# Heads' loop of two hybrid layers: a hand-written TensorE order and clamps on one engine

## Chip, core and metric

One core of one Trainium2 chip runs the whole program once. The metric is device microseconds of that core, median of several runs. TensorE is called PE below, VectorE DVE, ScalarE ACT, GpSimd POOL and the SyncE queue SP, as the profile names them.

## What is computed

The program is one transformer block followed by two "hybrid" layers, on 512 tokens of width 1024, all in float32. The change touches the state-space half of the hybrid layers only. Cut to that:

```python
def hybrid_layer(x, w_in, ...):
    q, k, v, z_attn, z_ssm, xbc, dt_raw = split(x @ w_in)
    attn = sliding_window_attention(q, k, v, sinks) * silu(z_attn)
    xs, bm, cm = split(silu(causal_depthwise_conv(xbc, conv_w, conv_b)))
    dt = softplus(dt_raw + dt_bias)
    y = ssd_chunked(xs, dt, -exp(a_log), bm, cm) + xs * d_skip
    ssm = gated_rmsnorm(y, z_ssm, ssm_norm_w)
    return layer_norm(ALPHA * x + concat(attn, ssm) @ w_out)

def ssd_chunked(xs, dt, a, bm, cm):          # 4 chunks of 128 tokens, 2 groups of 8 heads
    a_cs = cumsum(dt * a)                    # within a chunk
    xdt = xs * dt
    y_diag = (cm @ bm.T * exp(segsum(a_cs))) @ xdt
    states = bm.T @ (exp(a_cs[-1] - a_cs) * xdt)
    prev = scan(prev * exp(a_cs[-1]) + states)
    y_off = (cm @ prev) * exp(a_cs)
    return y_diag + y_off
```

## The kernel before

Activations lie transposed, channels on partitions and 512 tokens along the free axis. A product of one 128-channel output block ("unit") with the 1024-wide input is made in float32r with each operand split into a high and a low part: `proj` (L185) calls `mm3` (L142), 8 blocks x 3 = 24 PE products of 128x512 into one PSUM bank of the pool "mm" (4 banks): 16 with the high weights (L149, L150), then 8 with the low ones (L154). `weights` (L100) fetches a unit's 512 KB through SP (L104), casts it on ACT (`whi`, L107) and makes the rest on DVE in two pieces (`wlo`, L110); raw, high and low buffers are three each.

`hybrid` (L882) runs once per layer. `conv(j)` is one unit whose bank ACT copies into a tile "ht" (L900), DVE adds three shifted terms to (L902), ACT takes the tanh of (L211) and DVE combines (L905). `silu` (L908) is an ACT tanh and one DVE instruction (L911). Stages in order: four gates `zs` (half of them, for heads 0 to 7), dt, the convolutions of B and C, conv 0 and 1, the masked products `cb`, conv 2, 3 and 4, then the part at issue:

- `tokens(g)` (L1001), once for each group g of heads: for each of four chunks, four PE transposes into a bank "tr" (2 banks; L1007), two DVE products of that bank (`xdt` L1010, `xe` L1014), and, but for the last chunk, a state update: two full-precision float32 passes of 128x512 on PE into a bank "lg" (2 banks; L1016), for chunk 0 an ACT copy (L1019), else two DVE instructions (L1021, L1022). `xe` uses the two tiles "ht" that `conv` uses too.
- `decay_rows(j)` (L1025) issues four SP transfers that spread rows of cumulated sums from a scratch in HBM over partitions. That scratch is written by two transfers of the ACT queue (L951, L953).
- `decay(j)` (L1043), for each pair of heads j: per head four 128-wide clamps and one exponential (L1058), then a product with `cb` (L1059, first head on POOL, second on DVE). The clamp is an ACT Relu (L1057); for the first head of pairs 3 to 7 it is a DVE tensor_scalar (L1055), 20 of them in a layer.
- `heads(j)` (L1062): 16 PE products of 64 columns each (L1070) and 6 of 128 (L1076) into two banks "tr", then three DVE instructions (L1078 to L1080).
- The loop (L1094): for each j it fetches the weights of the next unit of `fill` (L1038), makes one unit (conv 5 to 7, then four gates), issues `decay(j + 1)`, `tokens(1)` at j = 3, `heads(j)`, the gating product (L1110), at j = 6 `gated_norm(0)` (L1082; a norm reduction on PE, L206, then L1087 and splits), and the sum of squares (ACT L199, POOL L200).

After the loop come two units of keys, the values (L1139 to L1141), `gated_norm(1)` and the attention.

The engines work through their queues in order. Who stands where in a queue is laid out at build time by a scheduler that takes what it reckons ready, earlier code first; only SP is kept in the order of the code (`manual_schedule`, L1312). So before the change the order of PE, too, is the scheduler's.

Of the kernel before, what the change touches and what calls it, by code (L numbers as in the profile page):

```python
# [11 lines left out]
ALU = mybir.AluOpType  # L12

P = 128
# [47 lines left out]
class Kern:  # L62
# [79 lines left out]
    def mm3(self, out, w, xs, m=P, start=True, stop=True, woff=0):  # L142
# [9 lines left out]
        for k, (xh, xl) in enumerate(xs):  # L152
            c = slice(woff + k * m, woff + (k + 1) * m)
            nc.tensor.matmul(out, wlo[:, c], xh, start=False, stop=stop and k == n - 1)  # L154

# [726 lines left out]
    def hybrid(self, L):  # L882
# [12 lines left out]
        def conv(j, tag, w=None):  # L895

            y, o = self.f("ht"), self.f(tag)
            cw = lambda w: cwh[:, w * 12 + j : w * 12 + j + 1]
            pt = self.proj(W[4 + j], h, w=w)
# [101 lines left out]
        def tokens(g):  # L1001

            for c in range(4):
                cc = slice(c * P, (c + 1) * P)
                ptx = self.ps("tr")
                for j in range(4):
                    nc.tensor.transpose(ptx[:, j * P : (j + 1) * P], xs[4 * g + j][:, cc], self.ident)  # L1007
                xdt[g, c] = self.f("G")
                o = c * 16 + 8 * g
                nc.vector.tensor_tensor(d3(xdt[g, c]), d3(ptx), bc(dtok, o), ALU.mult)  # L1010
                if c == 3:
                    break
                xe = self.f("ht")
                nc.vector.tensor_tensor(d3(xe), d3(ptx), bc(dend, o), ALU.mult)  # L1014
                pst = self.ps("lg")
                nc.tensor.matmul(pst, bt[c][:, g * P : (g + 1) * P], xe, start=True, stop=True)  # L1016
                prev = self.f("R")
                if c == 0:
                    nc.scalar.copy(prev, pst)  # L1019
                else:  # L1020
                    nc.vector.tensor_tensor(d3(prev), d3(prevs[g, c - 1]), bc(cdec, o), ALU.mult)  # L1021
                    nc.vector.tensor_tensor(prev, prev, pst, ALU.add)  # L1022
                prevs[g, c] = prev
# [10 lines left out]
        for j in range(2, 4):  # L1034
            xs.append(conv(j, "G"))
        xs.append(conv(4, "G"))

        fill = [9, 10, 11, 28, 29, 30, 31]  # L1038
        wn = self.weights(W[fill[0]])
        rows = [decay_rows(0), decay_rows(1)]  # L1040
        tokens(0)

        def decay(j):  # L1043

            dfs, ee = rows.pop(0)
            if j < 6:
                rows.append(decay_rows(j + 2))
# [46 lines left out]
        for j in range(8):  # L1094
            g = j // 4
            w = wn
            if j < 6:
                wn = self.weights(W[fill[j + 1]])
# [330 lines left out]
```

## Time and profile before

| | |
|---|---|
| median of 3 runs | 1650.42 us (1649.81 to 1650.58) |
| the profiled execution | 1650.6 us, its span 1648.8 us |
| PE busy | 1601.2 us, 97% of the span |
| DVE / ACT / POOL busy | 1140.7 / 805.5 / 212.4 us (69 / 49 / 13%) |
| mean granted clock of PE | 0.994 of full speed |

A PE instruction's recorded time runs to the end of its pipeline and overlaps the next one's, so what a product costs is read from start to start, not from its duration; a busy share near 100% can hide waiting.

In the rows further down, a row of busy time by stretch gives the stretch, its length, then the busy us and instruction counts of PE, PE's weight load, DVE, ACT and POOL, PE's granted clock, and the share and GB/s of the DMA engines. A row of a group gives line, engine, operation, names out<-in, shapes and count, then busy us and mean ns of one, then the engine's idle time before them and what ended it. A row of one line's durations gives min/median/max ns, and the first and last start. A row of the timeline gives start, length, and in brackets the idle time before.

### The profile page before, as it was taken

What the parts mean: (1) busy time and instruction counts of PE and PEld (TensorE: products, weight loads), DVE (VectorE), ACT (ScalarE), POOL (GpSimd) and SP (SyncE); (2) the same over time, 40 slices, a digit from 0 to 9 for tenths busy, and PEclk for the clock granted to TensorE, in tenths of its full rate; (3) what the DMA queues carried; (4) which work ended last, traced back from release to release, by engine and by line L of the source; (5) the groups of instructions that cost most, each with busy time, mean ns of one, the idle gap of its engine ahead of it and who ended that gap; (6) DMA issues with size and microseconds to landing.
All of it is one profiled execution on the core that took longest, in us unless ns stands there. A gap on an engine that the chain in (4) does not pass through costs nothing. (4 is left out here: it accounts for less than half of the span.)

```text
span 1648.8 us, 24498 instructions
## 1 busy us (share of the span) xinstructions
PE 1601.2 (97%) x9014; PEld 1358.7 (82%) x9014; DVE 1140.7 (69%) x2490; ACT 805.5 (49%) x1571; POOL 212.4 (13%) x251
## 2 busy tenths in 40 slices
PE   8999999999999999999999999999999989999996
PEld 5778888889898888888998778887998867888786
DVE  6779967547886455533767998765497799777447
ACT  4543245336863333323556556665355555666424
POOL 2000213000100000000000121211230022111131
PEclk9999999999999999999999999999999999999998
DMA  6522332243233323234636223211452522322133
GB/s 222 198 97 76 120 103 64 77 158 116 81 116 111 102 92 100 89 104 119 196 124 191 80 77 103 78 65 51 141 171 81 178 87 78 102 78 65 64 103 116
DMA packets 66233, 180.28 MB, mean 109 GB/s; under 512 B 7953, under 2 KB 19169, under 8 KB 66113
## 3 DMA queue, kind: packets, MB, share of 16 engines
q1 hardware_dynamic: 56320, 166.75, 31.8%
q10 hardware_dynamic: 9792, 11.96, 2.4%
q8 instruction: 71, 1.16, 0.3%
q14 instruction: 50, 0.40, 0.1%
HBM read 170.14 MB, written 9.06 MB: 109 GB/s over the span
## 5 line engine op out<-in xcount | busy, mean ns | idle before, releaser
L149 PE MATMUL psmm<-G,whi 128*128 128x512 f32 (+2 forms) x1244 | 479.2, 388 | 2.2 <-ACT whi L107 2.2
L110 DVE TENSOR_TENSOR wlo<-wraw,whi 128x512 fp32r<-128x512 f32 x515 | 358.8, 718 | 174.8 <-ACT whi L107 123.8
L150 PE MATMUL psmm<-G,whi 128*128 128x512 f32 (+2 forms) x1244 | 473.6, 384 | 0.0
L107 ACT CAST whi<-wraw 128x1024 fp32r<-128x1024 f32 (+3 forms) x262 | 267.7, 1024 | 339.7 <-PE psmm L150 272.3
L154 PE MATMUL psmm<-G,wlo 128*128 128x512 f32 (+2 forms) x1244 | 299.5, 382 | 0.0
L149 PEld LDWEIGHTS psmm<-G,whi 128*128 128x128 f32 (+1 forms) x1244 | 233.3, 188 | 50.3 <-issue 3.5
L150 PEld LDWEIGHTS psmm<-G,whi 128*128 128x128 f32 (+1 forms) x1244 | 233.2, 188 | 45.3 <-issue 1.5
L154 PEld LDWEIGHTS psmm<-G,wlo 128*128 128x128 f32 (+1 forms) x1244 | 228.2, 187 | 45.0
L149 PE MATMUL psmm<-R,whi 128*128 128x256 f32 (+1 forms) x684 | 210.4, 329 | 0.0
L150 PE MATMUL psmm<-R,whi 128*128 128x256 f32 (+1 forms) x684 | 210.1, 328 | 0.0
L149 PEld LDWEIGHTS psmm<-R,whi 128*128 128x128 f32 x684 | 130.0, 190 | 11.8 <-issue 0.3
L150 PEld LDWEIGHTS psmm<-R,whi 128*128 128x128 f32 x684 | 130.0, 190 | 11.5
L154 PE MATMUL psmm<-R,wlo 128*128 128x256 f32 (+1 forms) x684 | 130.3, 329 | 0.0
L154 PEld LDWEIGHTS psmm<-R,wlo 128*128 128x128 f32 x684 | 106.2, 190 | 11.5
L200 POOL TENSOR_TENSOR acc<-acc,sq 128x512 f32<-128x512 f32 (+1 forms) x42 | 53.0, 1261 | 475.4 <-ACT sq L199 475.3
L1176 ACT ACTIVATE w<-w,st 128x256 f32<-128x256 f32 (+1 forms) x128 | 59.9, 470 | 29.3 <-DVE st L1174 29.3
L211 ACT ACTIVATE sq<-ht 128x512 f32<-128x512 f32 (+1 forms) x48 | 29.4, 613 | 60.8 <-DVE ht L902 30.0
L902 DVE SCALAR_TENSOR_TENSOR ht<-psmm,cwh,ht 128x511 f32<-128x511 f32 (+2 forms) x72 | 53.4, 742 | 5.8 <-ACT ht L900 4.6
L836 DVE TENSOR_TENSOR sq<-psmm,G 128x512 f32<-128x512 f32 (+1 forms) x24 | 15.5, 646 | 56.0 <-PE psmm L154 56.0
L1172 DVE CUSTOM_DVE_ANT_0 w<-pslg,w,sinks 128x256 f32<-128x256 f32 (+1 forms) x128 | 51.5, 444 | 1.1 <-PE pslg L1167 0.6
L199 ACT ACTIVATE sq<-G 128x256 f32<-128x256 f32 (+1 forms) x76 | 35.1, 463 | 34.3 <-DVE G L1264 25.9
L1181 POOL TENSOR_SCALAR w<-w,st 128x256 f32<-128x256 f32 x64 | 37.9, 604 | 86.8 <-DVE st L1179 79.0
(332 smaller groups left out, 2597.3 us busy)
## 6 DMA issues: line engine op xcount, KB each, us to landing
wraw<-w_in SPq DMA_DIRECT2D x112, 512.0 KB, 3.4
wraw<-w_out SPq DMA_DIRECT2D x56, 512.0 KB, 3.8
wraw<-w_down SPq DMA_DIRECT2D x24, 512.0 KB, 3.5
wraw<-w_gate SPq DMA_DIRECT2D x22, 512.0 KB, 3.4
wraw<-w_up SPq DMA_DIRECT2D x22, 512.0 KB, 3.4
R<-acs SPq DMA_DIRECT2D x32, 256.0 KB, 5.7
wraw<-w_down SPq DMA_DIRECT2D x12, 384.0 KB, 3.7
wraw<-w_proj_attn SPq DMA_DIRECT2D x8, 512.0 KB, 3.4
```

Source lines behind the costliest of these rows:

```text
L107: nc.scalar.copy(hi[:, :n], raw[:, :n])
L110: nc.vector.tensor_tensor(lo[:, c], raw[:, c], hi[:, c].bitcast(F32), ALU.subtract)
L149: nc.tensor.matmul(out, whi[:, c], xh, start=start and k == 0, stop=False)
L150: nc.tensor.matmul(out, whi[:, c], xl, start=False, stop=False)
L154: nc.tensor.matmul(out, wlo[:, c], xh, start=False, stop=stop and k == n - 1)
L199: self.last_sq = nc.scalar.activation(t, src, AF.Square)
L200: (eng or nc.gpsimd).tensor_tensor(acc, acc, t, ALU.add)
L211: self.last_tanh = self.nc.scalar.activation(out, src, AF.Tanh, scale=scale)
L902: nc.vector.scalar_tensor_tensor(y[:, s:], pt[:, : S - s], cw(3 - s), y[:, s:], ALU.mult, ALU.add)
L1172: nc.vector.tensor_tensor_reduce(pr, pt, al[:, 256 - n :], 1.0, sink, ALU.add, ALU.max, mx[:, b : b + 1])
L1176: nc.scalar.activation(prs[b], prs[b], AF.Exp, bias=nm[:, b : b + 1], accum_out=sm[:, b : b + 1])
L1181: (nc.gpsimd if b % 2 else nc.vector).tensor_scalar(prs[b], prs[b], rc[:, b : b + 1], 1.0, ALU.mult, ALU.mult)
```

## The change

The loop becomes one stretch in which PE's order is that of the code. `unit` and `stream` hand out the 24 products of each of nine units (conv 4 to 7, four gates, the first unit of keys) one by one; `feed(n)` places n of them between a chunk's transposes (`tokens(g, c)`), its state update (`state(g, c)`) and the heads (`step(j)`). The clamps of `decay` are ACT Relus throughout. `xe` moves from tiles "ht" to tiles "rs" (two). Weights are fetched one unit ahead at the start of each unit; `decay_rows` are issued three pairs ahead, after `heads(j)`, and the first of them before the weights of conv 2. The products themselves, their number and their operands are the same.

```diff
@@ -152,6 +152,22 @@
         for k, (xh, xl) in enumerate(xs):
             c = slice(woff + k * m, woff + (k + 1) * m)
             nc.tensor.matmul(out, wlo[:, c], xh, start=False, stop=stop and k == n - 1)
+
+    def unit(self, w, xs):
+
+        whi, wlo = w
+        pt = self.ps()
+
+        def products():
+            n = len(xs)
+            for p in range(3 * n):
+                k = p // 2 if p < 2 * n else p - 2 * n
+                c = slice(k * P, (k + 1) * P)
+                lhs, rhs = (whi, xs[k][p % 2]) if p < 2 * n else (wlo, xs[k][0])
+                self.nc.tensor.matmul(pt, lhs[:, c], rhs, start=p == 0, stop=p == 3 * n - 1)
+                yield
+
+        return pt, products()
 
     def begin(self):
 
@@ -892,11 +908,12 @@
         cwh = self.s("cwh", (P, 60))
         nc.vector.tensor_scalar(cwh, self.vec[:, cw0 : cw0 + 60], 0.5, None, ALU.mult)
 
-        def conv(j, tag, w=None):
-
+        def conv(j, tag, pt=None):
+
+            if pt is None:
+                pt = self.proj(W[4 + j], h)
             y, o = self.f("ht"), self.f(tag)
             cw = lambda w: cwh[:, w * 12 + j : w * 12 + j + 1]
-            pt = self.proj(W[4 + j], h, w=w)
             nc.scalar.activation(y, pt, AF.Identity, scale=cw(3), bias=cwh[:, 48 + j : 49 + j])
             for s in (1, 2, 3):
                 nc.vector.scalar_tensor_tensor(y[:, s:], pt[:, : S - s], cw(3 - s), y[:, s:], ALU.mult, ALU.add)
@@ -998,29 +1015,31 @@
         xdt = {}
         prevs = {}
 
-        def tokens(g):
-
-            for c in range(4):
-                cc = slice(c * P, (c + 1) * P)
-                ptx = self.ps("tr")
-                for j in range(4):
-                    nc.tensor.transpose(ptx[:, j * P : (j + 1) * P], xs[4 * g + j][:, cc], self.ident)
-                xdt[g, c] = self.f("G")
-                o = c * 16 + 8 * g
-                nc.vector.tensor_tensor(d3(xdt[g, c]), d3(ptx), bc(dtok, o), ALU.mult)
-                if c == 3:
-                    break
-                xe = self.f("ht")
-                nc.vector.tensor_tensor(d3(xe), d3(ptx), bc(dend, o), ALU.mult)
-                pst = self.ps("lg")
-                nc.tensor.matmul(pst, bt[c][:, g * P : (g + 1) * P], xe, start=True, stop=True)
-                prev = self.f("R")
-                if c == 0:
-                    nc.scalar.copy(prev, pst)
-                else:
-                    nc.vector.tensor_tensor(d3(prev), d3(prevs[g, c - 1]), bc(cdec, o), ALU.mult)
-                    nc.vector.tensor_tensor(prev, prev, pst, ALU.add)
-                prevs[g, c] = prev
+        def tokens(g, c):
+
+            cc = slice(c * P, (c + 1) * P)
+            ptx = self.ps("tr")
+            for j in range(4):
+                nc.tensor.transpose(ptx[:, j * P : (j + 1) * P], xs[4 * g + j][:, cc], self.ident)
+            xdt[g, c] = self.f("G")
+            o = c * 16 + 8 * g
+            nc.vector.tensor_tensor(d3(xdt[g, c]), d3(ptx), bc(dtok, o), ALU.mult)
+            if c < 3:
+                xe[c] = self.f("rs")
+                nc.vector.tensor_tensor(d3(xe[c]), d3(ptx), bc(dend, o), ALU.mult)
+
+        def state(g, c):
+
+            o = c * 16 + 8 * g
+            pst = self.ps("lg")
+            nc.tensor.matmul(pst, bt[c][:, g * P : (g + 1) * P], xe.pop(c), start=True, stop=True)
+            prev = self.f("R")
+            if c == 0:
+                nc.scalar.copy(prev, pst)
+            else:
+                nc.vector.tensor_tensor(d3(prev), d3(prevs[g, c - 1]), bc(cdec, o), ALU.mult)
+                nc.vector.tensor_tensor(prev, prev, pst, ALU.add)
+            prevs[g, c] = prev
 
         def decay_rows(j):
 
@@ -1031,31 +1050,16 @@
                 nc.sync.dma_start(ee[64 * e_ : 64 * e_ + 64, P:], row[1:, P:].broadcast_to([64, S - P]))
             return dfs, ee
 
-        for j in range(2, 4):
-            xs.append(conv(j, "G"))
-        xs.append(conv(4, "G"))
-
-        fill = [9, 10, 11, 28, 29, 30, 31]
-        wn = self.weights(W[fill[0]])
-        rows = [decay_rows(0), decay_rows(1)]
-        tokens(0)
-
         def decay(j):
 
             dfs, ee = rows.pop(0)
-            if j < 6:
-                rows.append(decay_rows(j + 2))
             for e_, df in enumerate(dfs):
                 hd = 2 * j + e_
-                cut = e_ == 0 and j >= 3
                 for c in range(4):
                     cc = slice(c * P, (c + 1) * P)
                     at = atok[:, c * 16 + hd : c * 16 + hd + 1]
-                    if cut:
-                        nc.vector.tensor_scalar(df[:, cc], df[:, cc], at, 0.0, ALU.subtract, ALU.min)
-                    else:
-                        nc.scalar.activation(df[:, cc], df[:, cc], AF.Relu, bias=at, scale=-1.0)
-                nc.scalar.activation(df, df, AF.Exp, scale=1.0 if cut else -1.0)
+                    nc.scalar.activation(df[:, cc], df[:, cc], AF.Relu, bias=at, scale=-1.0)
+                nc.scalar.activation(df, df, AF.Exp, scale=-1.0)
                 (nc.vector if e_ else nc.gpsimd).tensor_tensor(df, df, cb[hd // 8], ALU.mult)
             return dfs, ee
 
@@ -1088,24 +1092,44 @@
                 cat[8 + i] = self.pair(t, "R")
 
 
+        fill = [8, 9, 10, 11, 28, 29, 30, 31, 0]
+        evict = [lambda pt, j=j: xs.append(conv(j, "G", pt)) for j in range(4, 8)]
+
+        def gate_evict(pt):
+            zs.append(self.f("R"))
+            silu(zs[-1], pt)
+
+        evict += 4 * [gate_evict] + [lambda pt: keys(pt)]
+        ahead = []
+
+        def stream():
+            for u, e in enumerate(evict):
+                pt, products = self.unit(ahead.pop(0), h)
+                if fill:
+                    ahead.append(self.weights(W[fill.pop(0)]))
+                for i, _ in enumerate(products):
+                    if i == 3 * KD - 1:
+                        e(pt)
+                    yield
+
+        fillers = stream()
+
+        def feed(n):
+            for _ in range(n):
+                next(fillers)
+
+
         cat = [None] * 16
         accs = []
-        ws = decay(0)
-        for j in range(8):
-            g = j // 4
-            w = wn
-            if j < 6:
-                wn = self.weights(W[fill[j + 1]])
-            if j < 3:
-                xs.append(conv(5 + j, "G", w))
-            elif j < 7:
-                zs.append(self.f("R"))
-                silu(zs[-1], self.proj(None, h, w=w))
-            nxt = decay(j + 1) if j < 7 else None
-            if j == 3:
-                tokens(1)
-            heads(j, *ws)
-            ws = nxt
+        ws = []
+
+        def step(j):
+
+            if j < 7:
+                ws.append(decay(j + 1))
+            heads(j, *ws.pop(0))
+            if j < 5:
+                rows.append(decay_rows(j + 3))
             y = xs[j]
             nc.vector.tensor_tensor(y, y, zs[j], ALU.mult)
             if j == 6:
@@ -1117,14 +1141,47 @@
 
         top, bot = slice(0, 64), slice(64, P)
         kt = []
-        for j in range(2):
-            pt = self.proj(W[j], h)
+
+        def keys(pt):
             ks = [[self.r("G") for _ in range(2)] for _ in range(2)]
             for (kh, kl), r, o in zip(ks, (top, bot), (bot, top)):
                 self.split(pt[r], kh[r], kl[r], 0.125)
                 for t in (kh, kl):
                     nc.scalar.dma_start(t[o].bitcast(F32), t[r].bitcast(F32))
             kt.append(ks)
+
+        xe = {}
+        rows = [decay_rows(0)]
+        for j in range(2, 4):
+            xs.append(conv(j, "G"))
+        ahead.append(self.weights(W[fill.pop(0)]))
+        rows += [decay_rows(1), decay_rows(2)]
+        ws.append(decay(0))
+        with self.tc.manual_schedule(engines={mybir.EngineType.PE}):
+            for g, lead in ((0, 20), (1, 20)):
+                feed(lead)
+                tokens(g, 0)
+                tokens(g, 1)
+                feed(10 - 2 * g)
+                state(g, 0)
+                tokens(g, 2)
+                feed(6)
+                state(g, 1)
+                tokens(g, 3)
+                feed(8 - 2 * g)
+                state(g, 2)
+                if g == 0:
+                    for n, j in ((8, 0), (24, 1), (22, 2)):
+                        feed(n)
+                        step(j)
+                else:
+                    for n, j in ((0, 3), (10, 4), (22, 5), (22, 6), (22, 7)):
+                        feed(n)
+                        step(j)
+                    feed(2)
+
+
+        keys(self.proj(W[1], h))
         vs = [self.f("G") for _ in range(2)]
         pv = [self.ps("mm") for _ in range(2)]
         for c in range(2):
```

## Rows read from the trace of the kernel before

**Rows 1.** Busy time by stretch: both layers' loops, then the first loop's middle

```profile
905.50:993.56 88.06, 81.20 (x464) 62.60 (x463) 80.93 (x135) 47.20 (x88) 21.62 (x14) 1.00 0.27 82
1309.97:1397.81 87.84, 81.34 (x465) 62.66 (x463) 80.90 (x132) 46.59 (x86) 20.44 (x14) 1.00 0.26 82
...
921.94:977.29 55.35, 50.83 (x300) 38.98 (x300) 54.10 (x96) 31.86 (x61) 13.73 (x9) 1.00 0.29 87
```

**Rows 2.** Waits of PE, first loop (905.50 to 993.56): total us, times, longest

```profile
PE pslg L1016 <- DVE ht L1014: 3.1, 2, 1.9
PE pstr L1007 <- DVE G L905: 1.6, 1, 1.6
PE pstr L1070 <- DVE G L1078: 1.2, 2, 0.9
PE psmm L149 <- ACT whi L107: 0.5, 1, 0.5
```

**Rows 3.** Timeline of PE in the first layer: start us, us, what, count, idle before

```profile
905.50 0.39 PE L149 MATMUL psmm<-G,whi 128*128 128x512 f32 x1
...
910.94 1.03 PE L1007 MATMUL pstr<-ident,G 128*128 128x128 f32 x8
...
911.73 0.48 PE L149 MATMUL psmm<-G,whi 128*128 128x512 f32 x1
...
917.04 1.06 PE L1016 MATMUL pslg<-ht,G 128*128 128x512 f32 x2
...
917.94 0.49 PE L1007 MATMUL pstr<-ident,G 128*128 128x128 f32 x3
...
921.94 1.10 PE L1016 MATMUL pslg<-ht,G 128*128 128x512 f32 x2 [1.87 <-DVE ht L1014]
...
962.55 1.09 PE L1070 MATMUL pstr<-R,G 128*64 128x128 f32 x16
...
964.26 0.47 PE L149 MATMUL psmm<-G,whi 128*128 128x512 f32 x1
...
969.92 1.09 PE L1070 MATMUL pstr<-R,G 128*64 128x128 f32 x16
...
1005.07 1.02 PE L206 MATMUL pstr<-acc,ones 128*128 128x512 f32 x2
1005.53 0.79 PE L149 MATMUL psmm<-G,whi 128*128 128x512 f32 x1
```

**Rows 4.** Groups, one line's durations, and timeline: DVE splits and clamps, a POOL product

```profile
L110 DVE TENSOR_TENSOR wlo<-wraw,whi 128x512 fp32r<-128x512 f32 x20 | 15.2, 785 | 0.9 <-ACT sq L199 0.9
...
L1055 DVE TENSOR_SCALAR R<-R,dtt 128x128 f32<-128x128 f32 x20 | 8.3, 439 | 0.0
...
L1055 DVE TENSOR_SCALAR R<-R,dtt x40: 269/280/1410, 931.4 to 1372.3; 128x128 f32<-128x128 f32 x40
...
936.28 1.28 DVE L1055 TENSOR_SCALAR R<-R,dtt 128x128 f32<-128x128 f32 x1
...
936.18 1.30 POOL L1059 TENSOR_TENSOR R<-R,R 128x512 f32<-128x512 f32 x1 [12.06 <-ACT R L1058]
```

**Rows 5.** ACT and POOL groups of the first loop

```profile
L107 ACT CAST whi<-wraw 128x1024 fp32r<-128x1024 f32 x10 | 10.3, 1042 | 4.0 <-PE psmm L150 4.0
L1057 ACT ACTIVATE R<-R,dtt 128x128 f32<-128x128 f32 x31 | 10.1, 389 | 0.0
L1058 ACT ACTIVATE R<-R 128x512 f32<-128x512 f32 x14 | 8.7, 626 | 3.1 <-DVE R L1055 2.9
...
L211 ACT ACTIVATE R<-psmm 128x512 f32<-128x512 f32 x4 | 2.4, 595 | 5.0 <-PE psmm L154 5.0
...
L1059 POOL TENSOR_TENSOR R<-R,R 128x512 f32<-128x512 f32 x7 | 9.9, 1412 | 36.8 <-ACT R L1058 36.8
```

**Rows 6.** Queues ahead of the first loop: the scratch's write, conv 2's first product

```profile
873.10 0.31 ACTq L953 DMA_DIRECT2D acs<-G  x1
...
894.23 0.48 PE L149 MATMUL psmm<-G,whi 128*128 128x512 f32 x1
```

## The prediction

> **What bounds the kernel now.** I first read the page's busy shares: PE is busy 97% of the span, so the time changes only where PE waits or where its work shrinks. This change alters no product, so I looked for waiting inside that 97%. The busy time by stretch [rows 1] shows the two loops as the places: 88.06 us in the first layer, from the end of conv 3's products to the first product of the values, and 87.84 us in the second. In both, DVE is busy 80.9 us, ACT about 47, POOL about 21. In the first loop's middle, 921.94 to 977.29, DVE is busy 54.10 of 55.35 us: there it is DVE that sets the pace, and PE, in order, stands behind it. The granted clock is 1.00 in all three rows, so no loss is the clock's.
>
> Then the waits of PE [rows 2]: state updates wait 3.1 us for `xe` from DVE, a transpose 1.6 us for conv 7's last DVE instruction, heads 1.2 us for DVE to leave a bank, one unit 0.5 us for ACT's cast. That is 6.4 us, but recorded durations overlap, so I worked out the loop's clean length from start to start [rows 3]. A unit of 24 products takes 910.94 - 905.50 = 5.44 us; eight transposes 911.73 - 910.94 = 0.79; a state update 917.94 - 917.04 = 0.90; a pair's heads 964.26 - 962.55 = 1.71; the norm reduction 1005.53 - 1005.07 = 0.46. The loop has 10 units (54.4), 32 transposes (3.2), 6 state updates (5.4), 8 pairs (13.7) and one reduction (0.5): 77.2 us. So 88.06 - 77.2 = 10.9 us is not products, in the second layer 10.6.
>
> Not all of this is waiting. A run of products that follows other work is longer than its count: 23 products took 917.04 - 911.73 = 5.31 us where 23 x 0.227 = 5.21, 24 after heads took 969.92 - 964.26 = 5.66 where 5.44 is clean [rows 3]. I take 0.16 for such a re-entry, the middle of 0.10 and 0.22. I count 12 in the loop now, 1.9 us; about 9 us a layer are waits.
>
> **The change part by part.**
>
> *PE's order.* By the feed counts, PE has 20 products (4.5 us) between conv 3's end and the first transposes, 10 (then 8 in group 1) between the first two chunks' transposes and the first state update, then 6 and 8 (6) before the next ones; about 22 before each pair, except 8 before pair 0, none before 3 and 10 before 4. Conv 7 ends at product 96, its transposes come after product 118 and pair 2: 22 x 0.227 + 1.71 = 6.7 us lie between, where none lay before and PE waited 1.6. The 1.87 us wait before the third state update [rows 3] gets 8 products, 1.8 us, in front of it. Pairs 0, 1 and the start of 2 ran back to back, which is the heads' wait of 1.2 us; now 24 and 22 products stand between. So the places that wait get cover. The price is more re-entries: I count 15 instead of 12, 2.4 us.
>
> The finer mixing has a rule against it. The Trainium skill (TensorEngine Tiling (Array Packing), Key Properties) says that a change of tiling mode drains TensorE, and heads write 64-partition halves. The rows above agree in sign, 0.22 us behind heads against 0.10 behind transposes, and the sum is made with their mean.
>
> *Clamps.* 20 clamps a layer leave DVE. They are busy 8.3 us, mean 439 ns, while their median over both layers is 280 ns [rows 4]: 20 x (439 - 280) = 3.2 us is stretch. One row shows why: a clamp of 1.28 us starts 0.1 us into a POOL product of 1.30 us and ends with it [rows 4]. So DVE is relieved of 5.1 us at least (if the stretch lands on its other instructions) and 8.3 at most; I take 7. In the loop's middle, where all 20 stand, 54.1 - 7 = 47.1 us of DVE work then stand beside six units, 16 transposes, four state updates and six pairs on PE, 32.6 + 1.6 + 3.6 + 10.3 = 48.1, with re-entries 49: DVE has less to do than PE there, by little.
>
> The Trainium skill (SBUF — State Buffer, Who interferes with whom) lets a tensor_scalar in a two-port mode and any DVE instruction with two SBUF inputs contend with a POOL instruction that reads SBUF. By it POOL's work keeps blocking other DVE instructions, and the relief would be the 5.1; the splits' mean of 785 ns here [rows 4] agrees with such blocking.
>
> *ACT.* It takes 20 Relus at 10.1 / 31 = 0.33 us [rows 5], 6.5 us a layer, on an engine busy 47 of 88 us [rows 1]. In the gate phase a pair costs ACT eight Relus (2.6), two exponentials at 0.62 (1.2), a cast (1.0), a tanh (0.6) and a square like it (0.6): 6.0 us against PE's 22 x 0.227 + 1.71 + 0.16 = 6.9. It fits, without room for disorder; I cost it at nothing, hidden behind those products. If the cover fails, a pair waits for the chain of the slower rival below.
>
> *Tiles, queues, fetches.* `xe` no longer shares the tiles "ht" with conv's accumulator, which only removes waits; I count nothing, since its wait cannot be told from DVE's. On SP the four transfers of `decay_rows(0)` move ahead of the weights of convs 2 to 4, and wait for the scratch that ACT's queue writes at 873.10 [rows 6]. Conv 2's products start at 894.23 [rows 6], 21 us later; four transfers, the fetch, cast and split stay well inside that: nothing. Inside the loop weights are asked for one unit (over 5.4 us) ahead behind four transfers at most. The order of ACT, DVE and POOL is again laid out by the scheduler, now around another PE order; that is bounded by nothing saved on one side and no waits left on the other, 10.9 us a layer apart, and I take the value worked out next.
>
> *What is left waiting.* In group 0, from the first transposes to the last state update, PE offers half of the transposes (1.6), 24 products (5.4) and two state updates (1.8): 8.8 us. DVE has there seven token products, conv 4's four instructions, one state's two and a unit's two splits, 15 instructions at some 0.65 us from start to start (the recorded means here are 0.68 to 0.79 and overlap by about 0.1): 9.8. So about 1 us is short; group 1 has two or four products less and a gate instead of a conv, and pair 3 follows at once: about 1 again. I take 2.2 us with the 0.2 of the rest.
>
> **Sum.** A loop takes 77.2 + 2.4 + 2.2 = 81.8 us: 6.3 less in the first layer (88.06 - 81.8), 6.0 in the second, 12.3 together. The profiled execution took 1650.6 us (span 1648.8), so 1638.3; the median of the runs is 0.2 lower, 1650.4, and gives 1638.
>
> **Rivals.** A measurement of this kernel can tell about 0.2%, 3.3 us, from no change.
>
> *DVE remains the wall.* If POOL's blocking moves over to other instructions and DVE keeps the 7.1 us that it idles in the loop now, the loop is 88.06 - 5.1 = 83.0 us at best, and with a split or a state late once more, 84: gains of 4 to 5 a layer, 1640.5 to 1643; down to 2 a layer, 1646.5, when the idle grows. For it: 98% busy in the middle. Against: 5.9 of its 7.1 idle us lie outside the middle (80.93 - 54.10 = 26.8 busy of 88.06 - 55.35 = 32.7 [rows 1]), where PE mostly had no need of it.
>
> *The waits only move.* The scheduler lays out ACT and DVE anew, and each of 6 state updates and 8 pairs waits 0.5 to 0.8 us: 7 to 11 us a layer, no gain, 1648 to 1653. For it: PE's queue is now rigid, where the scheduler had put ready work ahead. Against: every place of rows 2 gets products in front.
>
> *Slower: ACT's queue becomes the pacer.* Where a tanh that waits for a unit's last product stands in ACT's queue ahead of the Relus of the next pair, that pair's heads wait for tanh (0.6), Relus and exponentials (3.8) and the POOL product (1.4 [rows 5]): 5.9 us, less the products between. Units end at products 168 and 192, pairs 5 and 6 stand at 170 and 192, so the cover is 0 to 0.5 us. Two such places cost 11 us a layer against 6.2 saved: +5 each, about 1660. It decides from about one and a half places a layer. For it: the Relus moved over are those of exactly these pairs. Against: decay of a pair comes a whole step earlier in the code. The Trainium skill (ScalarE: Activation LUTs, Rules for kernel authors) tells authors to put relu and min on VectorE; the rows agree that the clamp is shorter there (a median of 280 ns [rows 4] against a mean of 389 on ACT [rows 5]), but ACT is the engine that has time.
>
> **How the numbers follow.** The forecast (1632 to 1640.5) has 0.52; DVE as the wall (1640.5 to 1646.5) 0.25; waits moved 0.10; slower 0.13. Small gains under 3.3 us fall in the third. So faster 0.77, same 0.10, slower 0.13. The low end: no waits and re-entries at 0.10 give 77.2 + 1.5 = 78.7 us a loop, 9.4 and 9.1 less, 1632. The high end takes in DVE as the wall and most of the waits moved, 1650.
>
> **What would show it.** In the changed profile, each loop should be about 82 us from conv 3's last product to the first of the values, with PE's waits for `xe` and L905 nearly gone, no L1055, and DVE busy some 74 us, under 95% in the middle. Runs of products behind heads should again be 0.1 to 0.2 us long. Wrong would be: heads waiting for POOL's or DVE's product of L1059 (ACT late), a unit waiting for its cast, or stretched two-input DVE instructions that make up for the clamps.

## The result, and the profile after

The change makes the kernel slower: the median goes from 1650.12 us (1649.33 to 1650.58, 4 runs) to 1660.38 us (1658.59 to 1661.57, 4 runs), a ratio of 1.0062, 95% interval 1.0044 to 1.0079. Forecast was 1638, range 1632 to 1650. The profiled execution after took 1658.59 us, span 1656.8.

The hybrid layer is best cut in three pieces. The first runs from conv-B/C's mask products (L979 before, L996 after) to the end of conv 3's products: the lead-in, which holds conv 2 and 3. The second is the loop, to the first product of the values; the third is the rest. The lead-in before, which [rows 1] do not hold, and then the pieces after, as busy time by stretch (start and end, length, then busy us and instructions of PE, PEld, DVE, ACT and POOL, PE's granted clock, DMA share and GB/s):

```profile
892.09:905.50 13.41, 13.41 (x72) 11.41 (x71) 10.49 (x16) 9.56 (x24) 1.30 (x1) 1.00 1.05 292
1296.66:1310.07 13.41, 13.41 (x72) 11.40 (x70) 10.49 (x16) 9.56 (x24) 1.29 (x1) 1.00 1.00 292
```

```profile
890.04:913.79 23.75, 16.20 (x72) 13.07 (x70) 13.37 (x21) 18.71 (x42) 3.85 (x3) 0.78 0.30 97
913.79:996.82 83.03, 80.27 (x464) 62.44 (x463) 71.37 (x114) 47.79 (x94) 14.23 (x10) 1.00 0.31 100
1298.64:1322.69 24.05, 16.50 (x71) 13.39 (x70) 13.38 (x21) 18.65 (x42) 3.85 (x3) 0.79 0.31 95
1322.69:1405.73 83.04, 80.28 (x463) 62.43 (x462) 71.24 (x113) 47.79 (x94) 14.21 (x10) 1.00 0.32 100
894.94:905.18 10.24, 5.21 (x13) 3.85 (x14) 5.08 (x8) 10.00 (x26) 1.88 (x2) 0.50 0.22 57
921.94:977.29 55.35, 54.97 (x325) 42.34 (x324) 48.45 (x81) 33.90 (x74) 11.65 (x8) 1.00 0.25 83
```

The loops are shorter: 83.03 and 83.04 us where [rows 1] have 88.06 and 87.84 (87.74 to the first product of the values), so 5.0 and 4.7 less. But the lead-ins, of which the forecast expected nothing, are 23.75 and 24.05 us where they were 13.41: 10.3 and 10.6 more. Together 21.0 - 9.7 = 11.3 us lost. The two profiled executions differ by less, 8.0 us, because outside these pieces the one of before is 3.3 us slower: it ran three stretches of 3.4 us at half clock there (from 98.9, 447.0 and 1235.5 us on) that the one of after does not have. Such stretches come and go: of the experiments' profiled executions some have one or two of them there, and some none. The medians differ by 10.3.

In the first lead-in, the same 72 PE instructions take 16.20 us of busy time where they took 13.41, and the granted clock is 0.78: for 10.24 us it is at 0.50, 1.2 GHz, as the row 894.94 to 905.18 shows. The other 7.5 us are idle. The first waits of PE over the whole span after, and last a line of before (total us, times, longest):

```profile
PE psmm L149 <- ACT whi L107: 10.5, 3, 4.6
PE pstr L1007 <- ACT G L1011: 5.8, 2, 2.9
PE psmm L698 <- DVE R L688: 5.2, 1, 5.2
PE pstr L222 <- DVE G L1082: 2.4, 2, 1.2
PE pstr L1023 <- DVE G L922: 2.3, 2, 1.2
...
PE psmm L149 <- ACT whi L107: 2.2, 3, 1.2
```

The first two lines are the two lead-ins', 4.6 and 2.9 us in each, but for one wait of 1.2 us for a cast far from the loops; before, the cast of a unit (L107) cost PE 2.2 us in the whole span, none of it in a lead-in, and L994, the copy that is now L1011, nothing. The third was there before too. The last two are the loop's (L222 is the norm's reduction, L1023 a token chunk's transposes, which were L206 and L1007). In the first loop's middle DVE is busy 48.45 of 55.35 us (54.10 in [rows 1]; in the stretch that lies as far behind the loop's start as that one did, 930.23 to 985.58, it is 47.44): it is no longer the wall. PE's timeline shows where the lead-in waits (start us, us, what, count, idle before):

```profile
891.82 0.60 PE L1007 MATMUL pstr<-ident,R 128*128 128x128 f32 x4
895.34 0.69 PE L1007 MATMUL pstr<-ident,R 128*128 128x128 f32 x2 [2.92 <-ACT G L1011]
900.65 0.80 PE L149 MATMUL psmm<-G,whi 128*128 128x512 f32 x1 [4.62 <-ACT whi L107]
901.25 0.63 PE L150 MATMUL psmm<-G,whi 128*128 128x512 f32 x1
901.68 0.63 PE L149 MATMUL psmm<-G,whi 128*128 128x512 f32 x1
```

Conv 2's first product starts 10.62 us after 890.04; before, 2.14 us after 892.09. The cast of its weights is late on ACT, whose timeline is, around that place, first after, then before:

```profile
888.02 0.63 ACT L227 ACTIVATE sq<-ht 128x512 f32<-128x512 f32 x1 [2.44 <-DVE ht L919]
890.24 0.78 ACT L917 ACTIVATE ht<-psmm,cwh 128x512 f32<-128x512 f32 x1 [1.59 <-PE psmm L154]
894.40 0.63 ACT L227 ACTIVATE sq<-ht 128x512 f32<-128x512 f32 x1 [3.38 <-DVE ht L919]
894.93 0.63 ACT L1011 COPY G<-pstr 128x256 f32<-128x256 f32 x2
...
896.34 1.27 ACT L1061 ACTIVATE R<-R,dtt 128x128 f32<-128x128 f32 x4
...
899.57 2.93 ACT L107 CAST whi<-wraw 128x1024 fp32r<-128x1024 f32 x3
```

```profile
878.53 1.06 ACT L107 CAST whi<-wraw 128x1024 fp32r<-128x1024 f32 x1 [2.84 <-PE psmm L150]
...
885.03 1.05 ACT L107 CAST whi<-wraw 128x1024 fp32r<-128x1024 f32 x1 [0.24 <-PE psmm L150]
...
890.48 1.05 ACT L107 CAST whi<-wraw 128x1024 fp32r<-128x1024 f32 x1 [2.84 <-PE psmm L150]
891.43 0.63 ACT L211 ACTIVATE sq<-ht 128x512 f32<-128x512 f32 x1
...
897.18 0.63 ACT L994 COPY G<-pstr 128x256 f32<-128x256 f32 x2
```

Before, the three casts stand in ACT's queue between the tanhs of the convolutions ahead (L211), the last of them just ahead of conv 0's. After, all three stand behind conv 1's tanh (L227), three copies of B's transposes (L1011), eight Relus (L1061) and two exponentials; ACT then takes them in one go at 899.57. It had time for them: idle 3.38 us ahead of that tanh alone, which waits for DVE. The copies for which PE waits 2.92 us are not late themselves: they start 4.89 us after the mask products' first, 5.09 before. Before, PE had conv 2's products to run until then; so this wait, too, comes from the late cast. Nor was the data missing. SP's queue after and, for the same three casts, before, and last the group of the three fetches after (KB each, median us from issue to landing):

```profile
869.85 0.33 SPq L1049 DMA_DIRECT2D R<-acs  x1
873.22 0.50 SPq L1050 DMA_DIRECT2D R<-acs  x1
873.77 0.58 SPq L1049 DMA_DIRECT2D R<-acs  x1
874.40 0.47 SPq L1050 DMA_DIRECT2D R<-acs  x1
874.98 1.47 SPq L104 DMA_DIRECT2D wraw<-w_in  x3
```

```profile
865.44 11.81 SPq L104 DMA_DIRECT2D wraw<-w_in  x3
```

```profile
wraw<-w_in SPq DMA_DIRECT2D x3, 512.0 KB, 5.8
```

The rows (L1049, L1050) wait on SP for the scratch, as foreseen, and the three weights are issued from 874.98, one behind the other, where before they went out singly between 865.44 and 877.25. After 5.8 us, by some 882, they are there: almost 18 us before the casts. So the transfers do fit, as the prediction worked out. What it did not see is that the cast, in ACT's in-order queue, moved with them.

### The profile page after: what moved, and what is told of

Read it like the earlier page. It is cut to its first block, busy times and chain, and to the rows that moved or that the text cites. A ratio compares the mean times of both kernels' runs of the same rounds, so it can differ in the third digit from the quotient of the medians.

```text
span 1656.8 us, 24485 instructions
## 1 busy us (share of the span) xinstructions
PE 1601.6 (97%) x9014; PEld 1358.6 (82%) x9014; DVE 1122.7 (68%) x2450; ACT 816.4 (49%) x1611; POOL 212.0 (13%) x251
## 5 line engine op out<-in xcount | busy, mean ns | idle before, releaser
L110 DVE TENSOR_TENSOR wlo<-wraw,whi 128x512 fp32r<-128x512 f32 x515 | 355.9, 713 | 168.8 <-ACT whi L107 143.5
L149 PE MATMUL psmm<-G,whi 128*128 128x512 f32 (+2 forms) x1100 | 423.7, 389 | 10.5 <-ACT whi L107 10.5
L107 ACT CAST whi<-wraw 128x1024 fp32r<-128x1024 f32 (+3 forms) x262 | 267.5, 1024 | 329.7 <-PE psmm L150 248.5
L150 PE MATMUL psmm<-G,whi 128*128 128x512 f32 (+2 forms) x1100 | 418.9, 384 | 0.0
L154 PE MATMUL psmm<-G,wlo 128*128 128x512 f32 (+2 forms) x1100 | 263.2, 381 | 0.0
L149 PEld LDWEIGHTS psmm<-G,whi 128*128 128x128 f32 (+1 forms) x1100 | 207.5, 189 | 54.0 <-ACT whi L107 11.4
L150 PEld LDWEIGHTS psmm<-G,whi 128*128 128x128 f32 (+1 forms) x1100 | 207.5, 189 | 40.3 <-issue 1.1
L154 PEld LDWEIGHTS psmm<-G,wlo 128*128 128x128 f32 (+1 forms) x1100 | 201.4, 187 | 39.6
L167 PE MATMUL psmm<-G,whi 128*128 128x512 f32 x288 | 74.2, 400 | 0.0
L919 DVE SCALAR_TENSOR_TENSOR ht<-psmm,cwh,ht 128x511 f32<-128x511 f32 (+2 forms) x72 | 53.6, 744 | 17.4 <-ACT ht L917 16.4
L167 PEld LDWEIGHTS psmm<-G,whi 128*128 128x128 f32 x288 | 52.7, 188 | 11.3 <-issue 1.0
L227 ACT ACTIVATE sq<-ht 128x512 f32<-128x512 f32 (+1 forms) x48 | 29.5, 614 | 59.1 <-DVE ht L844 28.6
```

Of the source, the lines that this page charges most:

```text
L107: nc.scalar.copy(hi[:, :n], raw[:, :n])
L110: nc.vector.tensor_tensor(lo[:, c], raw[:, c], hi[:, c].bitcast(F32), ALU.subtract)
L149: nc.tensor.matmul(out, whi[:, c], xh, start=start and k == 0, stop=False)
L150: nc.tensor.matmul(out, whi[:, c], xl, start=False, stop=False)
L167: self.nc.tensor.matmul(pt, lhs[:, c], rhs, start=p == 0, stop=p == 3 * n - 1)
L227: self.last_tanh = self.nc.scalar.activation(out, src, AF.Tanh, scale=scale)
```

## The experiments

Theory: the first `decay_rows` ahead of the weights on SP leads to an order of ACT in which the casts stand behind the tanhs and the Relus; everything lost is there, and the rest of the change gains. Rivals: the loop's own order loses time that the cuts above hide; the fetch itself is late; or the clamps, which are now all on ACT, make its queue late.

| run | median us | ratio to before, 95% interval | lead-ins us | loops us |
|---|---|---|---|---|
| before | 1650.12 | | 13.40, 13.41 | 88.06, 87.74 |
| after | 1660.38 | 1.0062, 1.0044 to 1.0079 | 23.75, 24.05 | 83.03, 83.04 |
| e1_rows_behind | 1638.80 | 0.9935, 0.9914 to 0.9956 | 13.41, 13.41 | 83.05, 83.06 |
| e2_before_rows_ahead | 1665.80 | 1.0092, 1.0077 to 1.0107 | 23.13, 23.33 | 86.43, 86.45 |
| e11_relus_behind_casts | 1653.25 | 1.0017, 1.0008 to 1.0027 | 19.74, 20.98 | 83.05, 83.03 |
| e7_fill | 1656.53 | 1.0038, 1.0025 to 1.0050 | 21.60, 21.59 | 83.03, 83.07 |
| e13_after_no_manual | 1653.29 | 1.0021, 1.0011 to 1.0031 | 23.79, 23.34 | 80.05, 80.06 |
| e3_clamps_dve | 1638.46 | 0.9930, 0.9915 to 0.9945 | 13.41, 13.42 | 83.22, 83.22 |
| e4_before_clamps_act | 1645.03 | 0.9972, 0.9962 to 0.9982 | 13.43, 13.43 | 86.43, 87.63 |
| e6_xe_ht | 1646.52 | 0.9976, 0.9964 to 0.9988 | 13.43, 13.43 | 84.87, 86.45 |
| e5_no_manual | 1633.73 | 0.9902, 0.9886 to 0.9917 | 13.42, 13.41 | 79.95, 80.02 |
| e8_leads | 1646.85 | 0.9983, 0.9973 to 0.9992 | 13.43, 13.43 | 87.03, 85.90 |
| e9_norm_later | 1637.50 | 0.9928, 0.9913 to 0.9942 | 13.41, 13.43 | 81.63, 81.64 |
| e10_lead23 | 1635.28 | 0.9917, 0.9902 to 0.9931 | 13.40, 13.43 | 80.88, 80.85 |

Lead-ins and loops are of each run's profiled execution, from the starts of their first products; each ratio is to runs of the kernel before made beside the run (medians 1649.92 to 1650.17). The second loops of e4, e6 and e8 hold a stretch of 3.4 us at half clock, e8's first one of 6.8.

### The place of the first rows' fetch

e1_rows_behind takes the changed kernel and puts only the first rows back:

```diff
-        rows = [decay_rows(0)]
         for j in range(2, 4):
             xs.append(conv(j, "G"))
         ahead.append(self.weights(W[fill.pop(0)]))
-        rows += [decay_rows(1), decay_rows(2)]
+        rows = [decay_rows(0), decay_rows(1), decay_rows(2)]
```

> The changed kernel with one edit: the first decay_rows goes back behind the weights of conv 2, conv 3 and conv 4 in the code, so on SP too. Queue theory (the loss lies ahead of the loop: those weights are cast late behind the Relus, PE waits 7.5 us a layer and its clock falls): the 10.3 us that conv 2 and 3 lost in each layer come back, 1660.4 - 20.6 = 1639.8, between 1637 and 1643, no half-clock stretch at the loops. Rival, the rigid order of PE is what costs: 1655 or more. Rival, the Relus moved to ACT hold up the casts: 1655 or more, casts still late.

e2_before_rows_ahead does the reverse, in the kernel before:

```diff
+        rows = [decay_rows(0)]
         for j in range(2, 4):
             xs.append(conv(j, "G"))
...
-        rows = [decay_rows(0), decay_rows(1)]
+        rows.append(decay_rows(1))
```

> The kernel before with only that one edit the other way round: the first decay_rows ahead of the weights of conv 2 to 4. Queue theory: PE waits for the casts ahead of conv 2 here too, 3 to 10 us a layer, 1656 to 1671. Rivals (rigid order, or Relus on ACT): neither is in this kernel, 1650, no change.

Both came as the theory has it. Without the moved fetch the lead-in is 13.41 us, the loop keeps its 83.05, and the kernel takes 1638.80 us, 0.8 from what had been forecast for the whole change. That closeness is in part luck: its loops give 9.7 us where 12.3 were forecast, and its profiled execution has none of the three stretches at half clock that the one of before has outside these pieces. With the moved fetch alone, the kernel before loses 9.7 and 9.9 us in the lead-ins and gets slower by 15.7 us in all (it gets back 1.6 and 1.3 in its loops). PE's waits in its first lead-in are the two of the changed kernel (L990 and L994 there are L1007 and L1011 after):

```profile
PE psmm L149 <- ACT whi L107: 3.7, 1, 3.7
PE pstr L990 <- ACT G L994: 2.9, 1, 2.9
```

On ACT its three casts come at 900.38, behind the last tanh, three copies, eight Relus and two exponentials, as in the changed kernel. So neither the written order nor the clamps are needed for the loss.

e11_relus_behind_casts leaves the rows ahead on SP and changes ACT's order alone: the first decay's instructions are issued behind the cast of conv 4's weights.

```diff
-        nc.scalar.copy(hi[:, :n], raw[:, :n])
+        self.cast = nc.scalar.copy(hi[:, :n], raw[:, :n])
...
-        ws.append(decay(0))
+        with self.tc.issue_after(self.cast.ins):
+            ws.append(decay(0))
```

> The changed kernel, the first decay rows still fetched ahead of convolution 2 to 4's weights, with one edit: ScalarE's first decay instructions (Relus and exponentials) are issued only behind the cast of convolution 4's weights. Theory (the order in ScalarE's queue is the cause, not the fetch, whose data had landed some 20 us before the cast): convolution 2's first product comes some 3 us sooner, the stretch ahead of the loop falls from 23.8 us to 20 or 21 or less, the loop stays at 83, time 1651 to 1655. Rival (the fetch of the weights, later on SP, is itself what is waited for): 23 to 24 us and 1660.

Conv 2 now starts 7.14 us after the mask products instead of 10.62, the lead-ins are 19.74 and 20.98 us and the time 1653.25: the theory's numbers. The fetch is as late as in the changed kernel, and conv 2 comes 3.5 us sooner by ACT's order alone. On ACT the casts now follow the third copy at once:

```profile
897.42 0.63 ACT L1011 COPY G<-pstr 128x256 f32<-128x256 f32 x2
898.30 0.37 ACT L1011 COPY G<-pstr 128x256 f32<-128x256 f32 x1 [0.25 <-PE pstr L1007]
898.57 2.94 ACT L107 CAST whi<-wraw 128x1024 fp32r<-128x1024 f32 x3
```

Of what is still lost, 6.3 and 7.6 us a layer, 5.0 are conv 2's later start, since the casts still stand behind the tanhs and copies, ahead of which they had been; the rest comes behind that start, where a part runs at half clock (3.4 us of the first lead-in, 6.8 of the second). A version with the rows ahead and the casts between the tanhs was not tried. Why the scheduler chose that order when the fetch moved is not shown either; that it follows the place of the fetch is.

### What the fallen clock costs by itself

e7_fill gives PE something to do in the two waits of the changed kernel: 36 more products whose result nobody reads.

```diff
         rows = [decay_rows(0)]
+        idle = self.ps()
+        for n in range(36):
+            nc.tensor.matmul(idle, h[n % 8][0][:, :P], h[n % 8][0], start=n == 0, stop=n == 35)
```

> The changed kernel, with 36 extra products of h with itself (each 128x512, one bank that nothing reads) on PE in each layer, ahead of conv 2, where PE waits: 14 before the last two transposes of B, 22 before conv 2's first product. The casts stay as late as they are. If the fall of the clock is a cost of its own: no half-clock stretch there, 24 products of conv 2 in 5.5 us instead of 7.7, conv 2 and 3 done 20.9 to 21.5 us after cb's start instead of 23.75, 5 us off in the whole: 1654 to 1657. Rival, only the wait costs: 1660, no gain.

The fillers fall into the waits (14 ahead of the last transposes, 22 behind them), conv 2 starts as late as in the changed kernel (10.69 us after the mask products, against 10.62), but the clock stays up, in the stretch from the mask products to conv 3's end:

```profile
891.02:912.62 21.60, 21.60 (x107) 18.16 (x106) 12.07 (x19) 17.07 (x39) 3.89 (x3) 1.00 0.34 107
```

The lead-ins are 21.60 and 21.59 us, so the half clock costs 2.15 and 2.46 us of the 10.3 and 10.6, and the late cast the other 8.2. (Conv 2 starts 0.07 and 0.33 us later than in the changed kernel, which the two smaller numbers leave out.) The kernel with 36 products more a layer is faster than the changed one by 3.9 us, by the ratios 4.0.

### Which parts of the change gain in the loop

All of these start from e1_rows_behind, but for e4, which starts from the kernel before. e3_clamps_dve puts the 20 clamps back on DVE:

```diff
-                    nc.scalar.activation(df[:, cc], df[:, cc], AF.Relu, bias=at, scale=-1.0)
-                nc.scalar.activation(df, df, AF.Exp, scale=-1.0)
+                    if e_ == 0 and j >= 3:
+                        nc.vector.tensor_scalar(df[:, cc], df[:, cc], at, 0.0, ALU.subtract, ALU.min)
+                    else:
+                        nc.scalar.activation(df[:, cc], df[:, cc], AF.Relu, bias=at, scale=-1.0)
+                nc.scalar.activation(df, df, AF.Exp, scale=1.0 if e_ == 0 and j >= 3 else -1.0)
```

> e1_rows_behind with the 20 clamps a layer back on DVE. If relieving DVE is worth something in the loop, slower than e1_rows_behind by 2 to 4 us a layer: 1643 to 1648. If the hand order alone does it: equal to e1_rows_behind within 2 us. Rival, ACT's added Relus cost time: faster than e1_rows_behind.

e4_before_clamps_act moves them alone, in the kernel before (`cut = False`):

> The kernel before with all clamps on ACT and nothing else. DVE-relief theory (my prediction's: DVE set the pace of the old loop and the 20 clamps were 7 of its us): its loops shrink by 2 to 4 us each, 1642 to 1646. Rival, the relief is worth nothing, as e3_clamps_dve says for the new order: 88 us a loop, 1650.

In the old order the move is worth 1.63 us in the first loop; the second holds a stretch at half clock. By the medians it is 5.1 us (1650.17 for the kernel before beside it), but executions of equal mean clock, 0.996, differ by some 3.3 us (1647.8 to 1648.8 before, 1644.3 to 1645.0 in e4), which is the 1.63 twice; the rest is not located. In the new order it is only 0.17 us a loop. The group of the clamps in e3's first loop shows why (busy us, mean ns, idle before):

```profile
L1062 DVE TENSOR_SCALAR R<-R,dtt 128x128 f32<-128x128 f32 x20 | 4.9, 278 | 0.0
```

They take 278 ns each, no longer 439 [rows 4], so no stretch is left, and PE's three waits in that loop are those of e1 within 0.1 us, none of them for a clamp. In e4's first loop the wait of 1.6 us at L1007 [rows 2] is gone and the others are there but for 0.2 us. The written order puts products in front of that same place, so the two parts are not to be added. The Trainium skill (ScalarE: Activation LUTs, Rules for kernel authors) would have these clamps on VectorE, and one is indeed shorter there (278 ns against 391 for a Relu after); by e3 and e4 the time depends on which engine PE stands behind.

e6_xe_ht puts `xe` back among the tiles "ht":

```diff
-                xe[c] = self.f("rs")
+                xe[c] = self.f("ht")
```

> e1_rows_behind with the tiles of xe back in ht, shared with conv's accumulator. If the separate tiles matter: state updates or conv 4's ACT copy wait, loop 84 to 87 us instead of 83.05, 1641 to 1647. If not: equal to e1_rows_behind, loop 83.0.

That costs 1.8 and 3.4 us a loop, 7.7 in the medians (0.9935 against 0.9976; the two were run in different sets). In both loops a state update waits for `xe` again, as in [rows 2], where e1 has 0.5; in the second loop, not in the first, the clock falls behind that wait. The wait (total us, times, longest), and the stretch at half clock as busy time:

```profile
PE pslg L1035 <- DVE ht L1029: 1.9, 1, 1.9
...
1323.40:1326.80 3.40, 3.40 (x8) 2.29 (x7) 0.69 (x1) 0.48 (x1) 0.66 (x1) 0.50 0.02 5
```

So of the 5.0 us that e1 gains in the first loop, these tiles account for 1.8 and the clamps for 0.2. The other 3.0 must lie in the code's new sequence with its feeds and fetches; no run takes these apart.

### The written order against the scheduler's

e5_no_manual keeps the code in the same sequence, but lets the scheduler order PE:

```diff
-        with self.tc.manual_schedule(engines={mybir.EngineType.PE}):
+        if True:
```

> e1_rows_behind with PE's order left to the scheduler again; the code, its feeds and everything else as there. If the hand-written order is what saves the waits: slower than e1_rows_behind by 2 to 5 us a layer, 1643 to 1650. If the order of the code (priorities) does it already: equal to e1_rows_behind within 2 us. Rival, the rigid order costs: faster than e1_rows_behind.

It is faster by 3.1 us a loop, and at 1633.73 us the fastest of all versions: the third outcome. So the gain in the loop does not need PE's order to be written by hand; the new sequence of the code is enough, and the fixed order costs. PE waits in its first loop, then in that of e1:

```profile
PE pstr L1023 <- DVE G L922: 0.2, 1, 0.2
```

```profile
PE pstr L222 <- DVE G L1082: 1.2, 1, 1.2
PE pstr L1023 <- DVE G L922: 1.1, 1, 1.1
PE pslg L1035 <- DVE rs L1029: 0.5, 1, 0.5
```

So I moved the pieces of the written order. e9_norm_later writes the norm, whose reduction waits for a bank that pair 6's L1082 leaves, 8 products later; e10_lead23 also feeds 23 products instead of 20 ahead of the first transposes:

```diff
-                    for n, j in ((0, 3), (10, 4), (22, 5), (22, 6), (22, 7)):
+                    for n, j in ((0, 3), (10, 4), (22, 5), (22, 6)):
                         feed(n)
                         step(j)
+                    feed(8)
+                    gated_norm(0, accs[0])
+                    feed(14)
+                    step(7)
```

```diff
-            for g, lead in ((0, 20), (1, 20)):
+            for g, lead in ((0, 23), (1, 20)):
...
-                    for n, j in ((8, 0), (24, 1), (22, 2)):
+                    for n, j in ((8, 0), (22, 1), (21, 2)):
```

> The version with the rows behind the weights, with one edit: the first group's gated norm is written after 8 of the 22 products between its last two pairs, not ahead of them. Theory (the written order stalls where a step of the chain is asked for before VectorE has it): the norm reduction's wait of 1.2 us and the slow first products beside it go, the loop falls from 83.05 us to about 81.6, twice, and the time from 1638.8 to about 1636. Rival (a written order costs these 3 us against the scheduler's wherever the pieces stand): loop 83, time 1638 to 1639.

> The version with the later norm, and the first group's lead raised to 23 products, one short of convolution 4's last, with feeds of 22 and 21 ahead of its first two pairs. Theory: the first transposes' wait for convolution 3's last instruction on VectorE falls from 1.3 us to about 0.6, loop about 81.0, time about 1635. Rival: as with the lead of 26, VectorE takes convolution 4's instructions ahead of the token products, the first state products wait some 4 us, loop 84 or more, time 1641 or more.

Loops of 81.63 and 80.88 us: 1.42 and another 0.75 less, as expected, and the rival, that a written order costs this wherever its pieces stand, falls. PE's waits in e10's first loop:

```profile
PE pstr L1023 <- DVE G L922: 0.4, 1, 0.4
PE pslg L1035 <- DVE rs L1029: 0.4, 1, 0.4
```

At 1635.28 us e10 cannot be told from e5 by the intervals; its loops are still 0.9 and 0.8 us longer. An earlier try, e8_leads, had gone too far, with leads of 26 and 18 where e1 has 20 and 20 (feeds of 22 and 20 follow, and the norm is late as in e9):

> e1_rows_behind with other feeds: 26 products instead of 20 ahead of group 0's transposes, 22 and 20 instead of 24 and 22 before pairs 1 and 2, 18 instead of 20 ahead of group 1; and gated_norm(0) after 8 of the 22 products between pairs 6 and 7. If three places of the hand order hold what e5_no_manual gained (a 1.3 us wait at the first transposes, about 0.8 around group 0's last state update, 1.5 at the norm's reduction): loop 79.5 to 80.5 us, 1632 to 1635, equal to e5_no_manual. Rival, a rigid order costs wherever its waits are put: loop 82 or more, 1637 or more.

It missed: 1646.85 us. The transposes did not wait any more, but then came this on PE:

```profile
912.37 2.52 PE L167 MATMUL psmm<-G,whi 128*128 128x512 f32 x10
919.40 2.08 PE L1035 MATMUL pslg<-rs,G 128*128 128x512 f32 x2 [4.50 <-DVE rs L1029]
```

and on DVE, meanwhile:

```profile
912.89 0.74 DVE L919 SCALAR_TENSOR_TENSOR ht<-psmm,cwh,ht 128x511 f32<-128x511 f32 x1
...
917.45 0.69 DVE L922 SCALAR_TENSOR_TENSOR G<-sq,ht 128x512 f32<-128x512 f32 x1 [0.69 <-ACT sq L227]
918.06 0.68 DVE L1026 TENSOR_TENSOR G<-pstr,dtt 128x512 f32<-128x512 f32 x1
918.66 0.68 DVE L1029 TENSOR_TENSOR rs<-pstr,dend 128x512 f32<-128x512 f32 x1
```

Conv 4 ends at product 24. With a lead of 26 it is finished ahead of the transposes, and in DVE's queue its four instructions (three L919, one L922), a split (L110) and a decay product (L1063) go ahead of the token products, which had their transposes since 912.6. With 23 they do not. In this wait, too, the clock fell, to 0.50 from 918.20 to 925.00: PE's two state products took 2.08 us, 1.02 in e1. The run made several edits at once; the norm's part of it is e9, which gained.

e13_after_no_manual, last, is the changed kernel, rows ahead, with PE's order left to the scheduler:

> The changed kernel with TensorE's written order taken away (the scheduler orders the products again), the first decay rows still ahead of the weights. Theory (two independent effects): stretch ahead of the loop about 23.5 us as in the changed kernel, loop about 80, time about 1654. Rival (the scheduler's order fills the wait for the weights with other products): stretch 13 to 18 us, time 1634 to 1645.

Lead-ins of 23.79 and 23.34 us and loops of 80.05 say that the two effects are independent: the scheduler's order of PE hardly fills the wait (76 instructions of PE in the first lead-in, where the written order has 72).

## Why the prediction was wrong

**The step that failed** is that on tiles, queues and fetches: "four transfers, the fetch, cast and split stay well inside that: nothing". The transfers did stay inside; the cast did not. I costed a move on SP's queue by its landing times and left ACT's queue as it had been, though shortly after I wrote that the order of ACT is laid out anew, and there I bounded it within the loop alone. The lead-in, 13.4 us with no wait in it, was in none of my sums. It measured +10.3 and +10.6 us: 8.2 for the late cast, 2.2 and 2.5 for the clock. That the clock could fall was not in the prediction: [rows 1] had shown 1.00 and I asked no further.

**The slower rival** had the right engine and, by chance, the right time (about 1660): ACT's queue with the wrong order in it. But its place was wrong (Relus behind a tanh, ahead of pairs 5 and 6, where PE has no such wait), and so was its condition. The casts were behind the Relus, ahead of the loop.

**PE's order**: that products in front of the waiting places cover them held, that the order has to be written by hand did not (e5). The forecast for a loop was 81.8 us; it measured 83.0. The re-entries were nearly right: 83.03 less 77.2 and less the places that e9, e10 and the waits show (1.4 at the norm, 1.3 at the first transposes, 0.5 at a state update) leaves 2.6 for 2.4; e5's 79.95, with 0.2 us of waits, leaves nearly as much. The waits were not: 3.2 for 2.2. I had put 1 us into group 1, where none is, and nothing on the norm's reduction, though the same view of before that gave [rows 2] had a fifth line, which I left out there and in the 6.4 us:

```profile
PE pstr L206 <- DVE G L1078: 0.5, 1, 0.5
```

**Clamps**: DVE was relieved by about what I took. Its busy time in the loop fell from 80.93 to 71.37 us, but two splits and a decay product of that only went ahead of the loop; in e1, which has as many of these in the loop as before, it is 72.97, so 8.0 less, 7 foreseen. The loop's middle fell to 88%, under the 95% named. That this is worth anything in the new order was wrong: e3 gives 0.17 us a loop. POOL's blocking, by which DVE was to remain the wall, did not move over: in e1's first loop the splits take 730 ns on the mean (785 in [rows 4]).

**ACT costed at nothing** held inside the loop (47.8 us busy of 83.0, and no wait of PE for ACT there). **`xe` at nothing** was wrong: e6 measured 1.8 us in the loop that has no half clock, over a third of the 5.0 gained there, and 3.4 in the other. I had folded it into the waits for DVE.

**The rivals on the faster side**: DVE as the wall gave 83.0 us a loop at best, which is what was measured, but by luck: DVE is not the wall, and what is left are, by the sum above, re-entries and three waits; the waits-only-move rival is excluded.

## What to carry to other kernels

When a fetch is moved, follow its data to the instruction that first reads it, and look where that instruction will stand in its own engine's in-order queue; a landing time well ahead of the need proves nothing when the reader's place moves too. Sum not only the stretch that a change is aimed at but the stretches ahead of it, up to the first instruction that it moves: here the edit that went along unnoticed cost twice what the edit in view gained. And after a hand-written order, build the same sequence of code once with the scheduler's: the three waits that it did not have, or hardly, named the places to mend.

## What was not expected of the hardware

PE's granted clock fell to 0.50, 1.2 GHz, for 10.24 us around waits of 2.92 and 4.62 us with two transposes between them, and for the last 4.5 us of these, from 900.65, PE already had conv 2's products to run: one every 0.43 us (901.25 to 901.68 in its timeline) against 0.23 at 2.4 GHz [rows 3]. In e11, with waits of 2.9 and 1.4 us, the mean clock of the first lead-in was 0.91 instead of 0.78; with fillers in both waits it was 1.00. So two waits cost 7.5 us as waits and over 2 us more by the clock, and products that nobody reads bought the latter back. In e6 a wait of 1.94 us was followed by 3.4 us at 0.50 in the second loop, and a wait of the same length in the first by none.
